# Keys and queries of heads 2, 4 and 6 by seven products ahead of attention 0, in place of gates; rotated operands split whole, stored and loaded as stacks

## The chip, the core and the metric

The kernel runs on one core of a Trainium2 chip, in one launch. The metric is the time of an execution on the device in microseconds (us); the median of three runs of the kernel before is 1436.19. The engines are TensorE (PE, with its weight loads as PEld), VectorE (DVE), ScalarE (ACT), GpSimd (POOL) and SyncE (SP), which issues the DMAs. Each executes its own instructions in order, and semaphores hold them together.

## The reference

A two-layer encoder trunk: 1024 tokens of width 1024, float32. Layer 0 is differential attention, layer 1 latent attention; each has an RMSNorm modulated by a conditioning vector, a SiLU gate, an output projection and a residual. The change lies in layer 0's projection and attention:

```python
# layer 0 (DA_HEADS 8, two parts of 64 per head, V of 128; D = SEQ = 1024)
proj = h @ w_in                                  # K, Q, V and the gate z, 1024 columns each
q, k, v, z = jnp.split(proj, [DA_WIDTH, 2 * DA_WIDTH, 3 * DA_WIDTH], axis=-1)
q = _rope(q.reshape(b, s, 2 * DA_HEADS, DA_QK_DIM), positions)
k = _rope(k.reshape(b, s, 2 * DA_HEADS, DA_QK_DIM), positions)
...
def block(qb):                                   # 128 queries
    sc = jnp.einsum('bqhcd,bkhcd->bhcqk', qb, k) * scale
    p = jax.nn.softmax(sc, axis=-1)
    p = p[:, :, 0] - lam * p[:, :, 1]
    return jnp.einsum('bhqk,bkhd->bqhd', p, v)
o = _rmsnorm(o, subln_g) * (1.0 - lambda_init)
o = o.reshape(b, s, DA_WIDTH) * jax.nn.silu(z)
return o @ w_out

def _rope(x, positions):                         # halves of 32 within each part of 64
    ...
    return jnp.concatenate([x1 * cos - x2 * sin, x2 * cos + x1 * sin], axis=-1)
```

## The kernel before

**Arithmetic.** Float32 is reached by splitting each operand into a high and a low part: `mm3` (L174 to L177) issues three matmuls per product, high x high, high x low, low x high. A split is an ACT cast to the high part and a subtraction for the low part, on POOL for weights (`split_raw`, L220 and L221, tiles `wh` and `wl`), on DVE for combinations and V. Operands are tiles of 128 partitions x 512 columns. The normalised input is `h0`, eight k-tiles by two token halves, each with a high and a low part (`h0h`, `h0l`).

**Head start.** `h0` is made, with the first half of V, K and Q of head 0 for the first token half beside it. The four last V tiles (`vacc`) are split and stored in memory (`store_v`, tiles `v_hl`, memory `vS`). Then K and Q of head 0 for the second token half, and the gate strip of head 6. A strip is one operand of one head: 1024 columns of weights by 128 rows, 16 steps of three matmuls. Raw K and Q of head 0 are parked in memory (`park`, `rS`).

**Pairs.** The gates of heads 0 to 5 are computed as three pairs of heads. A pair is a 2x2 block matrix product (two heads' weights, two halves of k) that takes seven products instead of eight: `z0_pair` (L931), with `product0` (L918: 12 matmuls into a PSUM tile `zacc`). It needs combinations of `h0` (`combos0`, L865: `tc`, `td` sums, `t1f` to `t4f`, each split into `t1..h`, `t1..l` and so on; L873 is the low part) and sums of weights (`z0_weights`, L902: L911 to L914 on DVE, then splits). `combos0` goes k by k, T1, T2, T4, T3 for each of the four k. PSUM tiles `acc` and `zacc` come in turn from five banks (`bank`, L117). Results go through SiLU (`gate_out`, L833) and are stored in `zS`.

**K1 and V.** After the pairs, the K strip of head 1 (16 steps, `Z_PRE`) and the second half of V, eight tiles of 24 matmuls (`v0_tile`, tiles `vps`). V's weights for it (`wv1`) are split there, with the low part on DVE (L554, L555). Beside it run the ropes of K and Q of head 0, the modulation products of layer 1 (DVE, `ada`, L441), and the first query tile (`V_LATE = 6`).

**Attention 0.** Per head and 128 queries: scores in PSUM (`s`, L1026, from the stacks `ks`, `qa`, `qb`), maximum (`nm`, DVE), exponential (`e`, ACT), the combination of both parts (L1034, DVE), transposes (`tr`), their splits (`pth` on ACT, `ptl` on DVE), then `pv` matmuls. Stream 0 supplies the strips of later heads as filler between them: `FILL0`, `FILL7` say how many steps go where. Its 15 strips are the rest of K and Q and the last gate.

**Ropes.** `rope` (L326) copies a strip out of PSUM (`rp_raw`), moves the 32-row blocks by four DMAs (`rp_sw`), multiplies by cosine and sine and adds (`rp_r`): three operations, on POOL but for head 0. Then `stack_k` (L358) and `stack_q` (L366) make the stacks: high and low parts of one 64-row half above each other, by two ACT casts and two POOL subtractions of 64 x 512, with four DMAs between halves for Q. What comes late is put in a side queue (`side.add`) whose jobs are called one per step (`side.tick`).

A scheduler places each engine's instructions by the order in which the code is written and its own priorities; `in_turn` and `behind` bind some of them. So the order on an engine is fixed when the kernel is built.

Of the kernel before, what the change touches and what calls it, by code (L numbers as in the profile page):

```python
# [11 lines left out]
F32 = mybir.dt.float32  # L12
# [27 lines left out]
FILL0 = ((1, 1, 1, 1, 1, 0), (1, 0, 1, 0, 1, 0)) * 3 + ((1, 1, 1, 1, 1, 0), (1, 0, 1, 0, 0, 0))  # L40
# [12 lines left out]
Z_PAIRS = 3  # L53
FILL7 = ((0, 1, 1, 1, 1, 0), (0, 1, 1, 1, 0, 0))
# [28 lines left out]
def trunk(ctx: ExitStack, tc: tile.TileContext, A, out):  # L83
# [54 lines left out]
    rS = dr.tile([2, 2, P, HF], F32, name="rS")  # L138
# [187 lines left out]
    def rope(rp, acc, half, scale, eng=G, add=V, parked=None):  # L326
# [5 lines left out]
        src = raw if parked is None else parked  # L332
        if parked is not None:
            SP.dma_start(raw, parked)
        elif scale == 1.0:
            S.copy(raw, acc)
        else:
            S.mul(raw, acc, scale)  # L338
        for q in range(4):
            SP.dma_start(sw[q * 32 : q * 32 + 32], src[(q ^ 1) * 32 : (q ^ 1) * 32 + 32])  # L340
# [17 lines left out]
    def stack_k(t, r):  # L358

        with behind("S"):  # L360
            S.copy(t[0:64, 0, :], r[0:64])
            S.copy(t[64:128, 1, :], r[64:128])
        in_turn(G.tensor_sub(t[64:128, 0, :], r[0:64], f32v(t[0:64, 0, :])))
        in_turn(G.tensor_sub(t[0:64, 1, :], r[64:128], f32v(t[64:128, 1, :])))

# [10 lines left out]

    def store_v(l, sp, acc, tt, fh, tag="vst", bufs=None):
        v = sp.tile([P, 2, HF], F32R, name="v_hl", tag=tag, bufs=bufs or VB[l])
# [376 lines left out]
    for tt in range(4):  # L755
        store_v(0, p1, vacc[tt], 4 + tt, 0, "xt", 6)

    def v0_tile(tt, fh, wv):
# [6 lines left out]
        if tt < V_LATE:  # L765
            store_v(0, p1b, acc, tt, fh)
        else:
            store_v(0, pm, acc, tt, fh, "ada", 3)
# [3 lines left out]

    def k_done(h):
        def f(acc, half, parked=None):
            rot, fin = rope(wp, acc, half, 1.0, *[G if h else V] * 2, parked)

            def g():
                t = a0a.tile([P, 2, HF], F32R, name="ks", tag="ks", bufs=4)
                stack_k(t, r.pop() if r else fin())
                KS.setdefault(h, [None, None])[half] = t  # L780

            r = []
            sum_ = [lambda: r.append(fin()), None] if h else []
            side.add(*[None] * ROT, rot, *[None] * (DEF - 1 - ROT), *sum_, g)
        return f

    def q_done(h):
        def f(acc, half, parked=None):
            rot, fin = rope(wp, acc, half, SC0, *[G if h else V] * 2, parked)

            def g():
                qa = a0a.tile([P, 2, HF], F32R, name="qa", tag="qs", bufs=4)
                qb = a0a.tile([P, 2, HF], F32R, name="qb", tag="qs", bufs=4)
                stack_q(qa, qb, r.pop() if r else fin())
                QS.setdefault(h, [None, None])[half] = qa, qb

            r = []
            sum_ = [lambda: r.append(fin()), None] if 0 < h < 5 else []
            side.add(*[None] * ROT, rot, *[None] * (DEF - 1 - ROT - (h == NH - 1)), *sum_, g)
        return f  # L800
# [8 lines left out]

    def z_done(h):  # L810
        def f(acc, half):
            GZ.setdefault(h, [None, None])[half] = silu_gate(wp, acc)
        return f

    def strip0(kind, h):
        return lambda: fetch_strip([A["w_s0"][kind, h, f] for f in range(2)], [4, 4])

    items = []
    for h in range(NH):
        items += [(strip0(1, h), h0, k_done(h)), (strip0(0, h), h0, q_done(h))]  # L820
# [1771 lines left out]
```

## Time and profile before

| what | us |
|---|---|
| runs | 1435.16, 1436.19, 1439.64 |
| profiled execution, its time | 1439.12 |
| its span | 1437.3 (mean granted clock 0.989) |
| head start | 0 to 81 |
| K0, Q0 second half, gate of head 6 | 81 to 103.1 |
| pairs | 103.1 to 180.1 |
| K1, second half of V | 180.1 to about 245 |
| first pv of attention 0 | 259.8 |

The profiled execution took 2.9 us more than the median, and 1.8 us of its time lie outside the span. The profile gives times in us from the span's start. A timeline row is: start, duration, engine, line, operation, output <- inputs, shape; in brackets the idle time of the engine just before it, and what ended it. A windows row is: window and length, busy time of each engine with the count of instructions, granted TensorE clock as a share, share of time in which the DMA engines worked, GB/s. A row of waits is: engine, what waited, line <- what it waited for: total, times, longest.

### The profile page before, as it was taken

The page shows a single profiled execution, that of the slowest core. Times are in us where ns is not written, and L with a number is a line of the kernel's source. Part 1 is how long each engine was busy: PE and PEld are TensorE (multiplying, and loading weights), DVE is VectorE, ACT ScalarE, POOL GpSimd, SP SyncE. Part 2 cuts the span into 40 slices and gives each one's busy share as a digit, 9 for nine tenths or more (in the row PEclk, how much of TensorE's full clock was granted, in tenths as well). Part 3 has the DMA queues.
Part 4 walks back from the last instruction along what each step waited for, and adds up shares of the span by engine and source line. Part 5 has one row for each costly group of instructions (what it writes and reads, how often), then busy time and mean ns, then how long its engine had stood idle before and what let it go on. Part 6 is the DMA issues. An engine that isn't in the chain of part 4 may idle for free.

```text
span 1437.3 us, 20898 instructions
## 1 busy us (share of the span) xinstructions
PE 1373.7 (96%) x7298; PEld 1141.9 (79%) x7298; DVE 986.8 (69%) x1392; ACT 760.2 (53%) x1369; POOL 773.2 (54%) x601
## 2 busy tenths in 40 slices
PE   8996989999999899999899899999999999999998
PEld 6774867878788788888787788887888888888886
DVE  7677564888787678777867886654655555555584
ACT  5533332656667566666754653334544454455554
POOL 5433434565598688876587232533032173753773
PEclk9997999999999999999999999999999999999999
DMA  9842267644544535444484236479544355565473
GB/s 342 285 128 74 73 216 221 202 135 125 147 131 156 172 110 173 149 138 120 145 322 154 67 72 204 170 248 269 160 132 120 107 135 194 193 220 191 134 269 117
DMA packets 154571, 241.50 MB, mean 168 GB/s; under 512 B 21217, under 2 KB 58209, under 8 KB 154466
## 3 DMA queue, kind: packets, MB, share of 16 engines
q1 hardware_dynamic: 154466, 240.18, 52.6%
q8 instruction: 57, 0.93, 0.3%
q14 instruction: 48, 0.39, 0.1%
HBM read 150.51 MB, written 66.53 MB: 151 GB/s over the span
## 4 chain that ended last, share of the span: by engine, by line
PE 60%; DVE 6%; ACT 3%; DMA 2%; issue 1%; POOL 1%; SPq 0%; POOLq 0%; ACTq 0%; DVEq 0%
PE s L2206 10%; PE tr L400 6%; PE acc L177 5%; PE acc L176 5%; PE s L1026 5%; PE acc L175 5%; PE pv L175 3%; PE pv L177 3%; PE pv L176 3%; PE oy L175 1%; PE oy L176 1%; PE oy L177 1%; PE zacc L177 1%; PE zacc L175 1%; PE zacc L176 1%
## 5 line engine op out<-in xcount | busy, mean ns | idle before, releaser
L402 ACT CAST pth<-tr 128x512 fp32r<-128x512 f32 x256 | 150.2, 587 | 250.2 <-PE tr L400 247.1
L403 DVE TENSOR_TENSOR ptl<-tr,pth 128x512 fp32r<-128x512 f32 x256 | 176.0, 687 | 144.7 <-ACT pth L402 139.9
L417 DVE TENSOR_REDUCE nm<-s 128x1 f32<-128x1024 f32 x192 | 233.6, 1217 | 18.5 <-PE s L1026 9.2
L221 POOL TENSOR_TENSOR wl<-wraw,wh 128x512 fp32r<-128x512 f32 (+2 forms) x65 | 83.9, 1292 | 204.4 <-ACT wh L220 155.0
L419 ACT ACTIVATE e<-s,nm 128x1024 f32<-128x1024 f32 x128 | 143.5, 1121 | 58.8 <-DVE nm L417 58.6
L400 PE MATMUL tr<-ident,e 128*128 128x128 f32 x1024 | 155.9, 275 | 6.0 <-DVE ptl L403 5.7
L400 PEld LDWEIGHTS tr<-ident,e 128*128 128x128 f32 x1024 | 121.2, 141 | 46.8 <-DVE ptl L403 25.8
L176 PE MATMUL pv<-ptl,vt 128*128 128x256 f32 x512 | 148.5, 290 | 0.7 <-DVE ptl L403 0.7
L175 PE MATMUL pv<-pth,vt 128*128 128x256 f32 x512 | 147.2, 288 | 0.4 <-ACT pth L402 0.4
L177 PE MATMUL pv<-pth,vt 128*128 128x256 f32 x512 | 144.6, 282 | 0.0
L175 PE MATMUL acc<-h0h,wh 128*128 128x512 f32 x264 | 108.8, 412 | 0.8 <-ACT wh L220 0.7
L177 PE MATMUL acc<-h0h,wl 128*128 128x512 f32 x264 | 104.5, 396 | 1.8 <-POOL wl L221 1.8
L176 PE MATMUL acc<-h0l,wh 128*128 128x512 f32 x264 | 104.2, 395 | 0.0
L221 POOL TENSOR_TENSOR wl<-zraw,wh 128x512 fp32r<-128x512 f32 (+2 forms) x39 | 56.8, 1461 | 85.5 <-ACT wh L220 82.2
L175 PEld LDWEIGHTS pv<-pth,vt 128*128 128x128 f32 x512 | 97.3, 190 | 3.8 <-ACT pth L402 1.9
L176 PEld LDWEIGHTS pv<-ptl,vt 128*128 128x128 f32 x512 | 97.6, 191 | 2.6 <-DVE ptl L403 1.1
L1026 PE MATMUL s<-ks,qa 128*128 128x512 f32 x256 | 86.0, 416 | 12.9 <-DVE e L1034 10.7
L1369 POOL TENSOR_TENSOR wol<-wol,woh 128x512 fp32r<-128x512 f32 x56 | 82.2, 1489 | 29.3 <-ACT woh L1368 26.4
L177 PEld LDWEIGHTS pv<-pth,vt 128*128 128x128 f32 x512 | 97.6, 191 | 0.2
L1026 PE MATMUL s<-ks,qb 128*128 128x512 f32 x256 | 83.7, 401 | 0.0
L1034 DVE SCALAR_TENSOR_TENSOR e<-s,z,e 128x1024 f32<-128x1024 f32 x64 | 82.2, 1284 | 2.2
L341 POOL TENSOR_TENSOR rp_r<-rp_raw,cosT 128x512 f32<-128x512 f32 x36 | 48.7, 1354 | 53.0 <-ACT rp_raw L338 52.3
(580 smaller groups left out, 3683.5 us busy)
## 6 DMA issues: line engine op xcount, KB each, us to landing
ada<-in_ada_ss SPq DMA_DIRECT2D x32, 512.0 KB, 6.1
vS<-v_hl SPq DMA_DIRECT2D x32, 512.0 KB, 6.0
vt<-vS SPq DMA_DIRECT2D x32, 512.0 KB, 4.8
wol<-tS SPq DMA_DIRECT2D x56, 256.0 KB, 5.4
wraw<-in_w_s SPq DMA_DIRECT2D x52, 256.0 KB, 2.8
tS<-ob SPq DMA_DIRECT2D x48, 256.0 KB, 2.1
rp_sw<-rp_raw SPq DMA_DIRECT2D x144, 64.0 KB, 2.0
bc_s<-bc_d SPq DMA_DIRECT2D x34, 256.0 KB, 3.9
```

The lines of the kernel that those rows point to most:

```text
L175: PE.matmul(psum, ah, bh, start=first, stop=False, skip_group_check=skip)
L176: PE.matmul(psum, ah, bl, start=False, stop=False, skip_group_check=skip)
L177: mm3.last = PE.matmul(psum, al, bh, start=False, stop=last, skip_group_check=skip).ins
L221: sub = (V if pair_of else G).tensor_sub(l_[:, :n], raw[:, :n], f32v(h_[:, :n]))
L400: transpose_p.last = PE.transpose(tr[:, j, :], p[:, kt * P : (kt + 1) * P], ident).ins
L402: mk["S"] = S.copy(pth[kh][:, :, dst], tr).ins
L403: mk["V"] = V.tensor_sub(ptl[kh][:, :, dst], tr, f32v(pth[kh][:, :, dst])).ins
L417: mk["V"] = V.reduce_max(nm, s_ps, axis=AX.X, negate=True).ins
L419: mk["S"] = S.activation(e, s_ps, AF.Exp, bias=nm, scale=1.0, accum_out=zs).ins
L1026: PE.matmul(s_ps[:, kc * HF : (kc + 1) * HF], src[:, c, ql], KS[h][kc][:, c, :], start=fst, stop=not fst)
L1034: combined.append(V.scalar_tensor_tensor(out=e0, in0=e1, scalar=z1[:, 0:1], in1=e0, op0=ALU.mult, op1=ALU.add).ins)
L2206: PE.matmul(s_ps[:, kc * HF : (kc + 1) * HF], lhs, rhs(kc), start=i == 0, stop=i == 4)
```

## The change

The pairs now compute K and Q of heads 2, 4 and 6 (`FRONT`), a head's K and Q being the two heads of the old pairs. The gate of head 0 takes the place of that of head 6 ahead of them. Stream 0 keeps 15 strips: K and Q of heads 1, 3, 5, 7 and gates 1 to 7 (`ORDER0`), with other filler counts. All gates are parked in `zS` and loaded for their head.

`rot_job` rotates a 128 x 512 operand as before and splits it whole: one cast on ACT, one subtraction for the low part; both parts go to memory (`hS`). `load_k` and `load_q` load the stacks from there by DMA. The ropes of heads 0 and 2 run on DVE during the pairs (8 jobs of 4 operations), those of heads 4 and 6 on POOL during V's second half (8 jobs), and those of the stream on POOL.

`combos0` does T1 and T2 of all k first, with the weight sums of the first pair after k = 1, then T3 of all k, then T4. Its temporaries get 12 tiles (8 before) and the weights 6 (8 before). The V tiles at the end of the head start are stored from `p1b` (tag `vst`, three buffers) and not from `p1` (tag `xt`, six). The second-half V weights are fetched and split at the end of the last pair, low part on POOL; they and V's stores live in `tp`, in the 16 buffers `tk` that hold the split combinations.

```diff
-FILL0 = ((1, 1, 1, 1, 1, 0), (1, 0, 1, 0, 1, 0)) * 3 + ((1, 1, 1, 1, 1, 0), (1, 0, 1, 0, 0, 0))
+FILL0 = ((1, 1, 1, 1, 1, 0), (1, 0, 1, 0, 1, 0)) * 4
+FILL6 = ((1, 1, 1, 1, 0, 0), (1, 0, 1, 0, 1, 0)) * 2 + ((1, 1, 1, 0, 1, 0), (1, 0, 1, 0, 0, 0)) * 2
-Z_PAIRS = 3
-FILL7 = ((0, 1, 1, 1, 1, 0), (0, 1, 1, 1, 0, 0))
+FRONT = (2, 4, 6)
+ORDER0 = ((1, 1), (0, 1), (2, 1), (1, 3), (2, 2), (0, 3), (2, 3), (1, 5), (2, 4), (0, 5), (2, 5), (1, 7), (2, 6), (0, 7), (2, 7))
+FILL7 = ((0, 1, 1, 1, 0, 0), (0, 1, 1, 1, 0, 0))
...
+    def rot_job(kind, h, half, eng, raw=None):
...
+        def first_():
+            b["r"] = rpt("rp_r")
+            turn_(eng.tensor_mul(b["r"], b["raw"], cosT[:, cs]))
+        def second():
+            turn_(eng.tensor_mul(b["sw"], b["sw"], sinT[:, cs]))
+            turn_(eng.tensor_add(b["r"], b["r"], b["sw"]))
+        def high():
+            with behind("S"):
+                S.copy(b["sw"].bitcast(F32R), b["r"])
+        def low():
+            turn_(eng.tensor_sub(b["raw"].bitcast(F32R), b["r"], b["sw"]))
+            for l_, t in enumerate((b["sw"], b["raw"])):
+                SP.dma_start(hS[kind][h][half][l_], t)
+        return fetch, first_, second, high, low
...
     for tt in range(4):
-        store_v(0, p1, vacc[tt], 4 + tt, 0, "xt", 6)
+        store_v(0, p1b, vacc[tt], 4 + tt, 0)
...
+    def load_k(h):
+        KS[h] = [a0a.tile([P, 2, HF], F32R, name="ks", tag="ks", bufs=4) for _ in range(2)]
+        for half, t in enumerate(KS[h]):
+            v = slots(1, h, half)
+            SP.dma_start(f32v(t[0:64]), v[:, 0::3])
+            for c in range(2):
+                SP.dma_start(f32v(t[64:128, c, :]), v[:, 2 - c])
...
+        for k in range(4):
+            V.tensor_sub(c_[k], d_[k], c_[k])
+            later(3, k, c_[k])
+            yield
+        for k in range(4):
+            bh, bl = parts[k][1]
+            V.tensor_sub(t2[k], bh, t2[k])
+            V.tensor_add(t2[k], t2[k], bl)
+            later(4, k, t2[k])
             yield
...
         if not p:
             side.flush()
+            add_jobs([(kind, 0, half) for kind in (1, 0) for half in range(2)] + [(kind, FRONT[0], half) for kind in (1, 0) for half in range(2)], V)
...
+    def split_v1(n):
+        for _ in range(n):
+            raw = wvraw.pop(0)
+            h_, l_ = tk()
+            S.copy(h_, raw)
+            G.tensor_sub(l_, raw, f32v(h_))
+            wv1.append((h_, l_))
...
+        if i < 2:
+            fetch_v1(2)
+        if i == 2:
+            split_v1(2)
+        if i == 3:
+            fetch_v1(2)
+            split_v1(2)
+            fetch_v1(2)
+            split_v1(4)
...
     stream0.step(Z_PRE)
+    add_jobs([(kind, h, half) for h in FRONT[1:] for kind in (1, 0) for half in range(2)], G)
...
-            if l == 0 and (h, half) >= (NH - 2, 1):
+            if l == 0:
                 hooks.append(lambda: hooks.append(scale))
...
+    def bring(h, i):
+        if h and i == 0:
+            load_q(h, 1)
+        if h < NH - 1 and i == 4:
+            load_k(h + 1)
+        if h < NH - 1 and i == 7:
+            load_q(h + 1, 0)
```

How this moves instructions, at three places. The first is the first pair, on **DVE, before**: the end of the combinations; `zs` and `zraw` (L911 to L914) are the weight sums, `z` the first add on a product.

```order
L892 TENSOR_TENSOR t4f<-h0h_0_143,t2f 128x512
L873 TENSOR_TENSOR t23l<-t2f,t23h 128x512
L893 TENSOR_TENSOR t4f<-t4f,h0l_0_144 128x512
L896 TENSOR_TENSOR t3f<-td,tc 128x512
L912 TENSOR_TENSOR zraw<-zraw 128x512
L873 TENSOR_TENSOR t43l<-t4f,t43h 128x512
L913 TENSOR_TENSOR zraw<-zs_1138,zraw 128x512
L873 TENSOR_TENSOR t33l<-t3f,t33h 128x512
L914 TENSOR_TENSOR zraw<-zraw 128x512
L936 TENSOR_TENSOR z_1165<-zacc,zu 128x512
```

**DVE, first pair, after**: lines L949 to L968 are the combinations, L937 the low parts (`tk`), L981 to L984 the weight sums.

```order
L981 TENSOR_TENSOR zs_1036<-zraw 128x512
L949 TENSOR_TENSOR tc<-h0h_1_188,h0l_1_189 128x512
L982 TENSOR_TENSOR zraw<-zraw 128x512
L950 TENSOR_TENSOR t1f<-tc,h0h_0_186 128x512
L937 TENSOR_TENSOR tk<-t1f,tk 128x512
L937 TENSOR_TENSOR tk<-t2f,tk 128x512
L937 TENSOR_TENSOR tk<-t1f,tk 128x512
L983 TENSOR_TENSOR zraw<-zs_1036,zraw 128x512
L951 TENSOR_TENSOR t1f<-t1f,h0l_0_187 128x512
L984 TENSOR_TENSOR zs_1037<-zraw 128x512
L937 TENSOR_TENSOR tk<-t2f,tk 128x512
L954 TENSOR_TENSOR td<-h0h_1_204,h0l_1_205 128x512
```

The weight sums now stand among the first combinations of k = 2, and no longer behind all combinations; the last of them (`zs_1037`) is the 14th row behind the fourth V tile (`v_hl`). The second place is the third pair, on **DVE, after** (before, only adds on `zacc`, gates and weight sums stood there):

```order
L393 TENSOR_TENSOR rp_sw<-rp_sw,sinT 128x512
L390 TENSOR_TENSOR rp_r<-rp_raw,cosT 128x512
L394 TENSOR_TENSOR rp_r<-rp_r,rp_sw 128x512
L401 TENSOR_TENSOR rp_raw<-rp_r,rp_sw 128x512
L393 TENSOR_TENSOR rp_sw<-rp_sw,sinT 128x512
L1010 TENSOR_TENSOR z_1623<-zacc,zu 128x512
L981 TENSOR_TENSOR zs_1537<-zraw 128x512
L982 TENSOR_TENSOR zraw<-zraw 128x512
L390 TENSOR_TENSOR rp_r<-rp_raw,cosT 128x512
L983 TENSOR_TENSOR zraw<-zs_1537,zraw 128x512
L394 TENSOR_TENSOR rp_r<-rp_r,rp_sw 128x512
L984 TENSOR_TENSOR zs_1538<-zraw 128x512
```

Rope operations (`rp_r`, `rp_sw`, `rp_raw`) now stand between the adds and among the third pair's weight sums. The third place is the stretch of K1 and V, on **POOL, before**, from the last splits of the pairs on:

```order
L221 TENSOR_TENSOR wl<-zraw,wh 128x512 x2
L221 TENSOR_TENSOR wl<-wraw,wh 128x512 x2
L346 TENSOR_TENSOR rp_sw<-rp_sw,sinT 128x512 x3
L221 TENSOR_TENSOR wl<-wraw,wh 128x512 x2
L363 TENSOR_TENSOR ks<-rp_r,ks 64x512
L364 TENSOR_TENSOR ks<-rp_r,ks 64x512
L363 TENSOR_TENSOR ks<-rp_r,ks 64x512
L364 TENSOR_TENSOR ks<-rp_r,ks 64x512
L371 TENSOR_TENSOR qb<-rp_r,qa 64x512
L372 TENSOR_TENSOR qb<-rp_r,qa 64x512
```

**POOL, after**: `tk<-wvr` are V's weights, `wl<-wraw` those of the strips K1 and the next.

```order
L224 TENSOR_TENSOR wl<-zraw,wh 128x512 x2
L1055 TENSOR_TENSOR tk<-wvr,tk 128x512 x3
L224 TENSOR_TENSOR wl<-wraw,wh 128x512
L1055 TENSOR_TENSOR tk<-wvr,tk 128x512 x4
L224 TENSOR_TENSOR wl<-wraw,wh 128x512
L1055 TENSOR_TENSOR tk<-wvr,tk 128x512
L224 TENSOR_TENSOR wl<-wraw,wh 128x512 x2
L390 TENSOR_TENSOR rp_r<-rp_raw,cosT 128x512 x2
L393 TENSOR_TENSOR rp_sw<-rp_sw,sinT 128x512
L394 TENSOR_TENSOR rp_r<-rp_r,rp_sw 128x512
L401 TENSOR_TENSOR rp_raw<-rp_r,rp_sw 128x512
L393 TENSOR_TENSOR rp_sw<-rp_sw,sinT 128x512
```

V's weight splits now stand ahead of and between K1's two, and the rope jobs follow in a chain. On **ACT, after**: `tk<-vps` are V's results, `rp_sw<-rp_r` the high parts of the rope jobs, `e` and `s` the exponentials.

```order
L412 CAST tk<-vps 128x512
L398 CAST rp_sw<-rp_r 128x512
L452 ACTIVATE s,z_2230<-s,nm 128x1024
L412 CAST tk<-vps 128x512
L398 CAST rp_sw<-rp_r 128x512
L452 ACTIVATE s,z_2335<-s,nm 128x1024
L398 CAST rp_sw<-rp_r 128x512 x4
L818 ACTIVATE rp_raw<-acc 128x512
L398 CAST rp_sw<-rp_r 128x512
L452 ACTIVATE e,zz<-s,nm 128x1024
L435 CAST pth<-tr 128x4x128 x2
```

and on **ACT, before**:

```order
L336 COPY rp_raw<-acc 128x512
L379 CAST v_hl<-vps 128x512
L336 COPY rp_raw<-acc 128x512
L369 CAST qa<-rp_r 64x512
L370 CAST qa<-rp_r 64x512
L379 CAST v_hl<-vps 128x512 x4
L419 ACTIVATE e,zz<-s,nm 128x1024
L379 CAST v_hl<-vps 128x512
L419 ACTIVATE s,z_2052<-s,nm 128x1024
L361 CAST ks<-rp_r 64x512
L362 CAST ks<-rp_r 64x512
L419 ACTIVATE e,zz<-s,nm 128x1024
```

Five of the rope casts now stand ahead of the second query tile's exponential (the row above the first `pth`), where the casts of stacks stood between V's results.

More of the change, by code (lines that the diff above doesn't have):

```diff
@@ L324, in step, with rope @@
                 side.tick()
[L326 removed]
+    def rope(rp, acc, half, scale, eng=G, add=V):
         cs = slice(half * HF, half * HF + HF)
@@ L764, in v0_tile @@
             mm3(acc, hh[:, c_], hl[:, c_], wv[k][0], wv[k][1], k == 0, k == KT - 1)
[L765 to L768, printed above, removed]
+            side.tick()
+        store_v(0, tp, acc, tt, fh, "tk", 16)
     KS, QS, GZ = {}, {}, {}
[L773 to L800, printed above, removed]
     def silu_gate(tp, acc):
@@ L980, in trunk, with late @@
-    assert not side.q and next(zw, None) is None
-    stT0.close()
+    def late(p, i):
+        if p + 1 < len(FRONT):
+            if i < 2:
+                z0_fetch(p + 1, ((i, 0), (i, 1)))
+            return
+        if i == 0:
+            z1raw = [raw_of(*ORDER0[0], f) for f in range(2)]
+            pre.append(z1raw)
+        if i < 2:
+            fetch_v1(2)
[6 more added lines that the diff above has]
+            split_v1(4)
@@ L1487, in extra0 @@
             side.flush()
+            for half in range(2):
+                load_gate(NH - 1, half)
             stW.close()
```

269 lines of the change are left out of this document (159 added, 110 removed).

## The prediction

> **What bounds the kernel now.** I read the page first: TensorE (PE) is busy almost throughout, so only the places where it stands still, or runs at a lower clock, can be won back.
>
> ```profile
> PE 1373.7 (96%) x7298; PEld 1141.9 (79%) x7298; DVE 986.8 (69%) x1392; ACT 760.2 (53%) x1369; POOL 773.2 (54%) x601
> ```
>
> Then the windows view, cut at the stages that the change touches: the seven-product pairs (103.1 to 181), K1 and the second half of V (181 to 240), most of attention 0 (300 to 700), and two cuts inside the first pair.
>
> ```profile
> 103.10:181.00 77.90, 63.01 (x257) 50.48 (x256) 51.46 (x74) 28.43 (x50) 33.96 (x22) 0.89 0.22 71
> 181.00:240.00 59.00, 53.54 (x230) 42.14 (x229) 29.75 (x42) 16.90 (x29) 25.77 (x18) 1.00 0.64 198
> 300.00:700.00 400.00, 381.05 (x2175) 319.31 (x2174) 310.78 (x444) 254.63 (x449) 292.65 (x238) 0.99 0.49 144
> 110.00:120.00 10.00, 3.77 (x10) 2.47 (x10) 10.00 (x17) 3.08 (x5) 0.00 (x0) 0.72 0.30 105
> 120.00:130.00 10.00, 4.85 (x11) 3.37 (x12) 5.96 (x11) 3.40 (x6) 4.19 (x3) 0.50 0.16 53
> ```
>
> Columns: length, then busy time of PE, PEld, DVE, ACT, POOL, granted clock, DMA. The pairs are the worst stretch of the three. In its first pair DVE is busy 10.00 of 10 us while PE works 3.77, and the granted clock is 0.72, then 0.50. The timeline says what a product costs and when the stage begins and ends:
>
> ```profile
> 103.12 0.39 PE L175 MATMUL zacc<-h0h,wh 128*128 128x512 f32 x1
> 105.84 0.39 PE L175 MATMUL zacc<-h0h,wh 128*128 128x512 f32 x1
> 109.97 0.50 PE L177 MATMUL zacc<-h0h,wl 128*128 128x512 f32 x1 [3.52 <-POOL wl L221]
> 125.01 0.79 PE L175 MATMUL zacc<-h0h,wh 128*128 128x512 f32 x1 [11.24 <-ACT wh L220]
> 180.11 0.39 PE L175 MATMUL acc<-h0h,wh 128*128 128x512 f32 x1
> ```
>
> The second row starts 12 matmuls after the first, so a product of 12 takes 2.72 us (0.227 each) and 21 take 57.1. The stage takes 180.11 - 103.12 = 77.0. So 19.9 us are lost: 14.8 in the two bracketed waits, some 5 at the low clock. Why the waits came:
>
> ```profile
> 84.65 0.69 DVE L883 TENSOR_TENSOR tc<-h0h,h0l 128x512 f32<-128x512 f32 x1 [1.77 <-DMA vS<-v_hl]
> 90.53 0.69 DVE L884 TENSOR_TENSOR t1f<-tc,h0h 128x512 f32<-128x512 f32 x1 [5.19 <-DMA vS<-v_hl]
> 120.02 0.68 DVE L893 TENSOR_TENSOR t4f<-t4f,h0l 128x512 f32<-128x512 f32 x1
> 120.62 0.68 DVE L896 TENSOR_TENSOR t3f<-td,tc 128x512 f32<-128x512 f32 x1
> 123.63 0.68 DVE L914 TENSOR_TENSOR zraw<-zraw 128x512 f32<-128x512 f32 x1
> 124.34 1.14 ACT L220 CAST wh<-zraw 128x512 fp32r<-128x512 f32 x2 [2.39 <-DVE zraw L914]
> ```
>
> DVE's combinations stood 6.96 us behind stores of V whose tiles lie in the same memory; they then run back to back, one per 0.60 us, with the weight sums last (L914 at 123.63, the cast at 124.34, PE at 125.01). And the 3.52 us wait:
>
> ```profile
> 103.42 6.50 POOL L221 TENSOR_TENSOR wl<-zraw,wh 128x512 fp32r<-128x512 f32 x1 [9.03 <-ACT wh L220]
> 108.11 0.67 DVE L888 TENSOR_TENSOR td<-h0h,h0l 128x512 f32<-128x512 f32 x1
> 108.72 0.67 DVE L807 SCALAR_TENSOR_TENSOR gz<-zth,acc 128x512 f32<-128x512 f32 x1
> 109.31 1.15 DVE L889 TENSOR_TENSOR t2f<-td,t1f 128x512 f32<-128x512 f32 x1
> 125.04 1.28 POOL L221 TENSOR_TENSOR wl<-zraw,wh 128x512 fp32r<-128x512 f32 x1 [15.12 <-ACT wh L220]
> ```
>
> POOL's split takes 1.28 us alone and took 6.50 here: it ended 1.2 us after DVE left its run of operations with two SBUF inputs for one whose input is in PSUM (L807), and the DVE operation behind that took 1.15 instead of 0.67.
>
> **The change, part by part.**
>
> ```profile
> L441 DVE CUSTOM_DVE_ANT_0 ada<-ada,c,vec 128x1024 f32<-128x1024 f32 x13 | 20.6, 1585 | 0.0
> ```
>
> This row (attention 0, by groups) prices the modulation products that stand among the rows counted next.
>
> *Combinations reordered.* V's stores now use a pool of their own, with three buffers for four tiles. Six combination rows run ahead of the fourth V tile, which has to wait for the first store. The first of the old waits ended at 84.65, the second at 90.53; I take about 86 for the fourth tile, and both as ends. The weight sums stand 14 rows behind it: 86 + 14 x 0.60 = 94.4, against 123.6 before and a need near 108. The 11.24 us wait goes, and so does the clock's fall after it. What is late next is the combination queue itself. Up to the add of the second product there are 47 DVE rows: 86 + 28 = 114, and with some five POOL splits let in between at 0.5 to 1.3 us each, 117 to 121. The last T4 split stands right behind that add, and products go to five banks in turn, so the seventh product needs both; its ideal start is 103.1 + 6 x 2.72 = 119.4. That leaves 0 to 4 us of stall, 2 taken.
>
> *32 rope operations on DVE inside the pairs* (heads 0 and 2, eight jobs of four). Before, DVE had room here: 51.46 busy of 77.90. From the second product's add to the weight sums of the third pair there are now 54 rows, 52 at 0.60 and two modulation products: about 34 us. That is 119 + 34 = 153. The splits of some 13 products come between them. Where a split enters beside an operation that reads PSUM, it costs DVE 0.5 (1.15 - 0.67); with no overlap it costs 1.28. So the sums end at 159 to 170. The 17th product needs them, and with 2 us of stall would be due at 103.1 + 16 x 2.72 + 2 = 148.6. Five products follow (13.6): the pairs end at 173 to 184 (180.11 before). Without any such delay, and were the rope rows overtaken, the end is 103.1 + 57.1 = 160.2. The price of this crowding is not in the old trace, since DVE was never full past the first pair, so I keep 160 to 184, and take 174, at the cheaper end of the crowded case: DVE also pauses for PE's products, and POOL enters then for nothing. Gain: 6 us (-20 to +4).
>
> The Trainium skill has a rule on this in "SBUF — State Buffer", section "Who interferes with whom": a DVE instruction with two SBUF inputs and a GpSimd instruction that reads SBUF share one port pair, and the second is fully blocked. The 6.50 against 1.28 agrees. Taken strictly it lets nothing overlap, which is the end at 184; the sum by it would be 10 us worse than mine.
>
> *V's weights split on POOL at the end of the last pair instead of on DVE after it.* Waits of the old K1 and V stretch:
>
> ```profile
> PE vps L175 <- DVE v_hl L380: 2.6, 2, 2.4
> PE vps L175 <- ACT wvh L554: 1.8, 1, 1.8
> PE vps L176 <- DVE wvl L555: 1.0, 1, 1.0
> 225.07 1.28 POOL L372 TENSOR_TENSOR qb<-rp_r,qa 64x512 fp32r<-64x512 f32 x1
> 226.44 1.29 POOL L341 TENSOR_TENSOR rp_r<-rp_raw,cosT 128x512 f32<-128x512 f32 x1
> 259.81 0.29 PE L175 MATMUL pv<-pth,vt 128*128 128x256 f32 x1
> ```
>
> The waits of 5.4 us go with their causes. In their place K1's second weight split stands behind seven V splits on POOL; at one POOL operation per 1.37 us (225.07 to 226.44) it is ready some 7 us after K1 starts, and K1's fifth step wants it after 4 x 3 x 0.227 = 2.7. So +4 against -5: net -1 (-5 to +5).
>
> *Ropes of heads 4 and 6 on POOL during V's second half.* With K1's two they are 10 jobs, 39 operations: 53 us at 1.37. The third job's low part waits for a cast that ACT has behind the sixth V tile, at T + 11 + 6 x 24 x 0.227 = T + 44 (T: end of the pairs); 28 operations follow, so POOL ends near T + 82. ACT has the last casts of these jobs ahead of the exponentials of attention's second tile, and the first pv behind those: about T + 83. Before it came at 259.81 = T + 79.7. DMA stores of the rotated halves stand ahead of V's stores and V's loads on SP's queue. PE gets some cover: one strip of 48 matmuls (10.9 us) now lies ahead of the first pv. I take +3 (-4 to +16).
>
> *Attention 0.* The stacks now come by DMA from memory half a head ahead, instead of by ACT casts and POOL subtractions just in time.
>
> ```profile
> PE s L1026 <- DVE e L1034: 10.4, 9, 4.8
> 499.93 1.10 PE L1026 MATMUL s<-ks,qa 128*128 128x512 f32 x2 [4.77 <-DVE e L1034]
> L371 POOL TENSOR_TENSOR qb<-rp_r,qa 64x512 fp32r<-64x512 f32 x14 | 18.0, 1284 | 9.7 <-ACT qa L369 9.7
> L363 POOL TENSOR_TENSOR ks<-rp_r,ks 64x512 fp32r<-64x512 f32 x14 | 18.0, 1287 | 41.3 <-ACT ks L361 40.6
> L361 ACT CAST ks<-rp_r 64x512 fp32r<-64x512 f32 x14 | 8.6, 613 | 7.9 <-POOL rp_r L348 7.9
> ```
>
> Four such POOL groups (4 x 18.0 us) and four ACT groups (4 x 8.6) go; about 14 whole-tile splits (18 and 9 us) come, and 14 gate products on DVE (9 us), which was 78% busy here (310.78 of 400). Neither engine is the bound, so only PE's waits count. Of the 19 us of waits in this stretch, 10.4 are for e; the longest (4.77) ended a rope chain that stood ahead of the exponential on ACT. I take 6 back (bounds -15 and +3, the last for the DVE work). The extra DMAs (from 1033 SP rows to 1173) I cost at nothing: the DMA engines are half busy there (0.49); were that cover gone, the loads have half a head, about 30 us.
>
> **Sum**, against the profiled execution of 1439.1: -6 - 1 + 3 - 6 = -10, or 1429. The median of the runs is 2.9 lower, 1436.2, so I forecast 1427.
>
> **Rivals.**
> - *More comes back* (0.2). Splits fit into DVE's pauses, the pairs end near 163, attention returns 8: -17 - 1 + 2 - 8 = -24, about 1413. For it: 20 us are plainly lost, and DVE could wait where PE has nothing to wait for. Against it: 90 DVE rows between 86 and 150.
> - *The stall moves and does not go* (0.2). Full blocking: the pairs end at 180 or later, with PE waiting for the third pair's weight sums instead of the first's: 0 - 1 + 3 - 5 = -3, about 1433 to 1438. The clock would fall again at that wait.
> - *Rope backlog delays attention 0: slower* (0.2). POOL's chain and the casts on ACT hold the first pv back. If the chain ends at T + 97 instead of T + 82 (each cast one V tile later, or V's loads landing behind the stores), PE runs out of the strip and waits 15 us more: -10 + 15 = +5, about 1441 to 1446. It decides from a first pv later than about T + 93. For it: ACT executes in order, four of those casts stand together ahead of an exponential. Against: V's work gives POOL 55 us of cover.
> - *The forecast* (0.4): 1421 to 1432.
>
> A rule of the Trainium skill bears on the second rival ("TensorE: Matmul & The Clock Gate", section "What's actually happening": after an idle window of about 3.4 us the gate passes half the pulses). The row of 0.50 behind the 11.24 us wait agrees.
>
> **Chances and range.** Under 0.3% (1431.9 to 1440.5 is no change, about what runs of this kernel can tell): all of the first rival and nearly all of the forecast's case make it faster, 0.55; the second rival and the forecast's upper edge are the same, 0.25; the third is slower, 0.2. The range leaves a tenth at each side: 1412 to 1443.
>
> **What would show it.** Right: no wait over 8 us in the first pair; 0 to 4 us before the seventh product; waits for POOL or ACT at the third pair's weights; first acc matmul of K1 at 170 to 177; a K1 wait of some 4 us for wl; first pv 80 to 86 us after that; waits for e under 6 us in all. Wrong: a pair stage under 62 us (crowding costs nothing) or over 77; a first pv past T + 93; or new waits in attention for ks or qa loads.

## The result, and the profile after

The change makes the kernel slower: median 1459.13 us (1458.04 to 1461.61, four runs) against 1437.91 for the kernel before beside it; ratio 1.0144, interval 1.0108 to 1.0181. The forecast was 1427. The profiled execution took 1461.6, its span is 1459.8 (before 1437.3): 22.5 us to explain.

The windows of the changed kernel, cut at the same stages (length, busy PE, PEld, DVE, ACT, POOL, clock, DMA share, GB/s):

```profile
103.00:181.00 78.00, 58.90 (x221) 44.73 (x220) 65.10 (x83) 27.26 (x49) 30.95 (x19) 0.87 0.59 193
181.00:240.00 59.00, 56.78 (x244) 46.52 (x243) 16.81 (x25) 14.76 (x27) 34.06 (x26) 0.97 0.69 190
240.00:300.00 60.00, 30.32 (x131) 23.82 (x130) 21.21 (x30) 16.46 (x29) 38.12 (x32) 0.77 0.82 249
300.00:700.00 400.00, 393.35 (x2273) 336.61 (x2273) 321.01 (x473) 237.68 (x422) 206.10 (x172) 0.99 0.71 204
150.00:160.00 10.00, 2.84 (x6) 1.83 (x7) 8.08 (x12) 3.11 (x5) 2.95 (x2) 0.67 0.82 264
```

In 300 to 700, most of attention 0, PE is busier than before (393.35 of 400 against 381.05). In the pairs it is less busy (58.90 of 78.00 against 63.01 of 77.90), and at the start of attention it works half of 60 us. The timeline of PE, with its larger waits and the ends of the stages (the first acc is K1's first matmul):

```profile
118.46 0.47 PE L178 MATMUL zacc<-tk,wh 128*128 128x512 f32 x1 [2.79 <-DVE zth L844]
157.03 0.79 PE L178 MATMUL zacc<-h0h,wh 128*128 128x512 f32 x1 [7.25 <-ACT wh L223]
171.46 0.80 PE L178 MATMUL zacc<-h0h,wh 128*128 128x512 f32 x1 [5.29 <-ACT wh L223]
188.69 0.39 PE L178 MATMUL acc<-h0h,wh 128*128 128x512 f32 x1
287.91 1.22 PE L1129 MATMUL s<-ks,qa 128*128 128x512 f32 x2 [25.55 <-ACT e L452]
299.29 0.35 PE L178 MATMUL pv<-pth,vt 128*128 128x256 f32 x1 [3.55 <-DMA vt<-vS]
```

And where the first matmul of the out projection stands, in the tile view of `oy` (min/median/max ns, first to last start), before and after:

```profile
L175 PE MATMUL oy<-woh,oah x136: 278/393/501, 694.8 to 1428.3; 128*128 128x512 f32 x132, 128*128 128x256 f32 x4
```

```profile
L178 PE MATMUL oy<-woh,oah x136: 278/393/505, 716.2 to 1450.5; 128*128 128x512 f32 x132, 128*128 128x256 f32 x4
```

So the difference at the end of attention is 21.4 us, in three parts. The pairs end at 188.69 instead of 180.11: +8.6. From there to the first pv: 110.6 instead of 79.7, +30.9. From the first pv to the out projection: 416.9 instead of 435.0, -18.1. After it the two kernels run alike (+22.2 at the last `oy`). Little of the -18.1 is work done earlier. These two windows rows, the first of the kernel before, count the strip matmuls (`acc`) from the pairs' end to the first pv (they have no column for POOL):

```profile
180.10:259.80 79.70, 20.19 (x83) 15.25 (x82) 0.00 (x0) 1.78 (x3) 1.00 0.71 224
188.68:299.28 110.60, 24.44 (x96) 18.85 (x95) 0.00 (x0) 2.39 (x4) 0.86 0.77 225
```

There were 83 and are 96 now. The 13 more are about 3.0 us at the 0.227 us that a matmul takes.

Why the large wait: the timeline of ACT and of POOL shows a chain of rope jobs, and the exponential that PE needs behind its last cast.

```profile
221.79 0.62 ACT L398 CAST rp_sw<-rp_r 128x512 fp32r<-128x512 f32 x1 [0.98 <-POOL rp_r L394]
261.86 0.62 ACT L398 CAST rp_sw<-rp_r 128x512 fp32r<-128x512 f32 x1 [7.66 <-POOL rp_r L394]
267.62 0.62 ACT L398 CAST rp_sw<-rp_r 128x512 fp32r<-128x512 f32 x1 [5.15 <-DMA rp_sw<-rS]
286.14 0.62 ACT L398 CAST rp_sw<-rp_r 128x512 fp32r<-128x512 f32 x1 [3.18 <-POOL rp_r L394]
286.66 1.11 ACT L452 ACTIVATE e<-s,nm 128x1024 f32<-128x1024 f32 x1
```

The first of the ten casts came at 221.79, the last at 286.14: 7.15 us a job on average, against 5.5 (four POOL operations at 1.37) in the forecast. And why the third pair waits, from SP's queue:

```profile
150.49 0.32 SPq L403 DMA_DIRECT2D hS<-rp_raw  x1
150.86 0.45 SPq L383 DMA_DIRECT2D rp_raw<-rS  x1
151.36 1.84 SPq L386 DMA_DIRECT2D rp_sw<-rS  x4
153.29 0.84 SPq L920 DMA_DIRECT2D zraw<-in_w_s  x2
156.36 1.26 ACT L223 CAST wh<-zraw 128x512 fp32r<-128x512 f32 x2 [1.00 <-DMA zraw<-in_w_s]
```

The first raw weights of the third pair are fetched at 153.29, behind rope stores (`hS`) and the loads that follow them; their cast comes at 156.36 and PE's matmul at 157.03. The rest is fetched at 159.40. The second wait, of 5.29 us, ends with the sums of these weights, and these stand on DVE behind an add on a product of the same pair, for which DVE waits until PE has made it:

```profile
166.28 0.69 DVE L1010 TENSOR_TENSOR z<-zacc,zu 128x512 f32<-128x512 f32 x1 [3.70 <-PE zacc L180]
166.89 0.68 DVE L981 TENSOR_TENSOR zs<-zraw 128x512 f32<-128x512 f32 x1
```

### The profile page after: what moved, and what is told of

The parts are those of the page before. It is cut to its first block, busy times and chain, and to the rows that moved or that the text cites. A ratio compares the mean times of both kernels' runs of the same rounds, so it can differ in the third digit from the quotient of the medians.

```text
span 1459.8 us, 20961 instructions
## 1 busy us (share of the span) xinstructions
PE 1379.5 (94%) x7298; PEld 1152.0 (79%) x7298; DVE 993.7 (68%) x1408; ACT 735.9 (50%) x1331; POOL 706.6 (48%) x553
## 4 chain that ended last, share of the span: by engine, by line
PE 51%; DMA 3%; DVE 3%; issue 2%; ACT 1%; POOL 1%; SPq 0%; POOLq 0%; DVEq 0%; ACTq 0%
PE s L2313 10%; PE tr L433 5%; PE acc L178 4%; PE acc L180 4%; PE acc L179 4%; PE pv L178 3%; PE pv L179 3%; PE pv L180 3%; PE s L1129 3%; PE zacc L178 1%; PE zacc L180 1%; PE zacc L179 1%; PE oy L180 1%; PE oy L178 1%; PE oy L179 1%
## 5 line engine op out<-in xcount | busy, mean ns | idle before, releaser
L224 POOL TENSOR_TENSOR wl<-zraw,wh 128x512 fp32r<-128x512 f32 (+2 forms) x36 | 51.6, 1440 | 77.2 <-ACT wh L223 57.3
L1129 PEld LDWEIGHTS s<-ks,qa 128*128 128x128 f32 x256 | 42.9, 192 | 41.5 <-ACT e L452 27.6
```

What stands on the lines that cost most here:

```text
L224: sub = (V if pair_of else G).tensor_sub(l_[:, :n], raw[:, :n], f32v(h_[:, :n]))
L1129: PE.matmul(s_ps[:, kc * HF : (kc + 1) * HF], src[:, c, ql], KS[h][kc][:, c, :], start=fst, stop=not fst)
```

## The experiments

Single profiled executions are named as such; the others are medians with the ratio to the kernel before beside them.

**1. Where the loss at the start of attention comes from.** The rope jobs of heads 4 and 6 in V's second half were first moved away, then done on another engine.

```diff
-    add_jobs([(kind, h, half) for h in FRONT[1:] for kind in (1, 0) for half in range(2)], G)
+    # in gen_strips0, at the first step of a gate strip:
+            if kind == 2 and gate_jobs:
+                add_jobs(gate_jobs[:2], G)
```

> The ropes of heads 4 and 6 leave V's second half and run two jobs per gate strip of stream 0 (gates 1 to 4); nothing else changes. Theory: PE's wait of 25.5 us ahead of the first pv comes from five rope casts that stand ahead of an exponential on ACT, each waiting for the chain of rope jobs on POOL. Then that wait goes (under 5 us), the first pv comes 80 to 86 us after the pairs' end (110.6 in the changed kernel), the time is 1432 to 1438. Rival: V's stores and loads or the full DMA engines (0.82 in that stretch) hold attention back: 15 us or more of the wait stay, 1448 or more.

Measured 1467.83, ratio 1.0216 (1.0185 to 1.0248). The wait goes, as theory had it: the first pv comes 74.4 us after the pairs' end.

```profile
189.09 0.39 PE L178 MATMUL acc<-h0h,wh 128*128 128x512 f32 x1
263.47 0.28 PE L178 MATMUL pv<-pth,vt 128*128 128x256 f32 x1
```

But the time does not fall, because attention 0 loses more than was won: PE is busy 369.88 of 400 there. The expected time failed; the place of the wait did not.

```diff
-    add_jobs([(kind, h, half) for h in FRONT[1:] for kind in (1, 0) for half in range(2)], G)
+    add_jobs([(kind, h, half) for h in FRONT[1:] for kind in (1, 0) for half in range(2)], V)
```

> The ropes of heads 4 and 6 stay in V's second half, on DVE instead of POOL. If POOL's four operations of 1.3 us set the pace of the chain (about 7 us a job), DVE at 0.6 ends it some 20 us sooner: wait ahead of the first pv 5 to 10 us, 1438 to 1444. If the two jobs in flight are paced by their round trip through memory (five loads issued, 3 us to land, store 2.3), a job still takes 5.5 to 6 us: wait 15 to 20, 1449 to 1455.

One execution: 1451.1. The wait falls from 25.5 to 19.0 only, so POOL's speed accounts for a quarter of it. Late in that chain some of DVE's rows wait for loads:

```profile
285.62 1.22 PE L1129 MATMUL s<-ks,qa 128*128 128x512 f32 x2 [19.04 <-ACT e L452]
275.89 0.69 DVE L393 TENSOR_TENSOR rp_sw<-rp_sw,sinT 128x512 f32<-128x512 f32 x1 [2.13 <-DMA rp_sw<-rS]
278.82 0.69 DVE L390 TENSOR_TENSOR rp_r<-rp_raw,cosT 128x512 f32<-128x512 f32 x1 [0.90 <-DMA rp_raw<-rS]
```

A job takes three of six buffers, so two jobs are in flight; each must be loaded, rotated, cast and stored before its buffers serve the next but one. No run with more buffers was made, so their share in the wait is not shown.

```diff
+            if high_on is G:
+                in_turn(G.tensor_copy(b["sw"].bitcast(F32R), b["r"]))
+                return
             with behind("S"):
                 S.copy(b["sw"].bitcast(F32R), b["r"])
```

> The ropes of heads 4 and 6 stay in V's second half as in the changed kernel; only their high casts move from ACT to POOL (8 copies of 1.3 us), so that ACT's exponential no longer stands behind them. If the order on ACT alone held attention back, the wait for e goes and the first pv comes near 265 to 270: 1435 to 1442. If SP's queue is a second gate (V's last stores and V's loads stand behind the stores of these jobs), the wait moves to vt<-vS or stays, first pv 290 or later: 1450 to 1462.

One execution: 1457.5, wait 22.9. With the casts off ACT two other waits stand ahead of the same exponential:

```profile
280.98 0.60 ACT L821 ACTIVATE rp_raw<-acc 128x512 f32<-128x512 f32 x1 [25.70 <-POOL rp_raw L404]
285.07 1.11 ACT L455 ACTIVATE e<-s,nm 128x1024 f32<-128x1024 f32 x1 [3.50 <-DMA vS<-tk]
```

The raw copy of the next strip needs one of the six rope buffers, which the chain frees; and the exponential's own tile lies where V's split results were, so it waits for V's stores, which stand on SP behind the rope stores. Moving the rope stores off SP too:

```diff
-                SP.dma_start(hS[kind][h][half][l_], t)
+                (G if eng is G else SP).dma_start(hS[kind][h][half][l_], t)
```

> The ropes of heads 4 and 6 in V's second half, high casts on POOL, and now all stores of POOL's rope jobs issued from POOL's own DMA queue, so that V's stores and loads no longer stand behind them on SP. Theory: with the casts on POOL two gates were left, the third V-store wait on SP (ACT's exponential waited for vS<-tk) and the raw copy of the next Q strip on ACT, which waits for a rope buffer that POOL's chain frees (25.7 us). If SP was the larger one, the first pv comes near 265 to 275: 1436 to 1446. If the rope buffers are, it stays at 285 or later: 1450 to 1460.

One execution: 1464.1, 6.6 more than the execution without; the raw copy waits 25.1 us for its buffer, the first pv is at 301.1. So with eight jobs there, neither the casts on ACT nor the stores on SP alone hold attention back; the chain does, through whichever wait is left.

**2. Why the pairs end late.**

```diff
-            SP.dma_start(raw, A["w_s0"][1 - m, FRONT[p], f])
+            (S if p else SP).dma_start(raw, A["w_s0"][1 - m, FRONT[p], f])
```

> The raw weights of the second and third pair are fetched by ACT's DMA queue instead of SP's; nothing else changes. Theory: in the third pair PE waits 7.25 and 5.29 us because the fetch stands on SP behind stores of the rope jobs. Then the pairs end at 174 to 180 (188.7 in the changed kernel), the time is 1445 to 1451. Rival, the crowding of DVE and POOL that was forecast: the weight sums come no sooner, the pairs end at 184 or later, 1455 to 1460.

Measured 1453.91, ratio 1.0111 (1.0091 to 1.0131). The pairs end at 172.09, even below the expected 174, so the fetch on SP's queue cost 16.6 us there. PE's matmuls stand in the same order in both kernels, but DVE's operations do not: with the weights there sooner, the scheduler put the third pair's sums ahead of the adds that they stood behind (first row below; 166.89 in the changed kernel). The 16.6 us are both together. The first pv gains only 5.8: the rope chain is the later arm now, and PE waits 35.3 us for it. The time, 1445 to 1451 expected, gains less for that reason.

```profile
144.28 1.40 DVE L981 TENSOR_TENSOR zs<-zraw 128x512 f32<-128x512 f32 x1 [1.85 <-DMA zraw<-in_w_s]
172.09 0.39 PE L178 MATMUL acc<-h0h,wh 128*128 128x512 f32 x1
281.71 1.22 PE L1129 MATMUL s<-ks,qa 128*128 128x512 f32 x2 [35.29 <-ACT e L452]
293.54 0.55 PE L178 MATMUL pv<-pth,vt 128*128 128x256 f32 x1 [3.90 <-DMA vt<-vS]
```

> As the first of these, and head 2's ropes leave the pairs: its Q in V's second half on POOL (two jobs), its K in gate 1; heads 4 and 6 in gates 2 to 5. So DVE has 16 rope operations in the pairs, not 32, and SP fewer stores ahead of the third pair's raw weights. Theory: both losses of the changed kernel go, the pairs end at 165 to 174, the first pv 80 to 86 us later, 1414 to 1424. Rival: the pairs are held by the combinations and their port alone: they end at 183 or later, 1430 to 1436.

Its edit takes head 2's four jobs out of the pairs (`add_jobs` there for head 0 only) and gives gates 1 to 5 two jobs each but for two in V's half. Measured 1471.47, ratio 1.0238 (1.0204 to 1.0271). The pairs end at 177.77 (165 to 174 expected, with the raw weights still on SP) and the first pv is at 256.96, but ten jobs in gates cost still more than eight. The expected time failed for the same reason as in the first run.

**3. What a rope job costs in attention 0.** First suspicion: a cast directly behind its last rope operation stops ACT.

```diff
-                add_jobs(gate_jobs[:2], G)
+                side.add(fA, None, None, fB, a1, a2, None, b1, hA, lA, b2, None, None, hB, lB)
```

> As the run with the ropes of heads 4 and 6 in the gate strips, but the two jobs of a strip are interleaved so that two to three stream steps lie between the last rope operation and the high cast (none lay there). Theory: that run lost in attention 0 because ACT stood 4 to 5 us before such casts, with exponentials behind them. Then the waits for e fall from 14.8 us to under 7, attention 0 is busy as in the changed kernel (PE over 390 of 400 in 300 to 700), and the time is 1428 to 1438. Rival: more work on POOL, ACT or the DMA queue in attention 0 costs by itself: PE stays under 380 of 400, 1455 or more.

One execution: 1467.9. PE's waits for `e` from ACT between 300 and 700 fell from 10.3 to 6.4 us, but waits for `qb` rose from 0.9 to 6.1 and PE is busy 368.23 of 400. So the suspicion does not explain the loss.

> The gapped gate strips and the raw weights on ACT's queue together. Theory: both losses of the changed kernel are gone and its gain in attention 0 stays. Pairs end near 172, first pv near 250, 1410 to 1422. Rival: the gains do not add, because attention 0 then waits for ropes: 1430 or more.

Measured 1459.60, ratio 1.0130 (1.0104 to 1.0155): pairs end at 172.48, first pv at 252.57, and attention 0 gives it all back (370.14 of 400). Nor did other gates help:

> Raw weights on ACT's queue; of the eight rope jobs of heads 4 and 6 two (K of head 4) stay in V's second half, two each go to gates 1, 3 and 5, which stand ahead of K strips, with the gap before the high casts. Theory: in the two gapped runs attention 0 lost because rope jobs in gates 2 and 4 delayed the side queue of the Q strips right behind them, whose stacks are wanted three query tiles later (PE waited 9.9 and 5.7 us for qa, 6.1 and 2.2 for qb). Then those waits fall under 5 us in all, first pv near 252, 1420 to 1435. Rival: any rope job in attention 0 costs: waits for e, qa and vt as before, 1450 or more.

Measured 1465.27, ratio 1.0172 (1.0143 to 1.0201). With only two jobs in V's half PE still waits 9.0 us ahead of the first pv, behind an exponential that waits for V's stores, which follow rope stores on SP:

```profile
254.92 1.11 ACT L452 ACTIVATE e<-s,nm 128x1024 f32<-128x1024 f32 x1 [12.49 <-DMA vS<-tk]
```

The sibling with four jobs in V's half:

> The same with four jobs (K and Q of head 4) in V's second half and two each in gates 1 and 3. The chain of six jobs, at 7 us each from about 200, ends near 245, before the second tile's exponential. Theory: first pv 250 to 258 and less in attention 0: 1416 to 1432. Rival (any backlog in V's second half holds V's stores back): first pv 265 or later, 1440 or more.

One execution: 1457.5, first pv 273.0. What these share stands in the waits of SP's queue, here of the gapped run with raw weights on ACT's queue, in 300 to 700 (what waited, for what: us, times, longest):

```profile
SPq L403 <- ACT rp_sw L398: 61.5, 18, 9.7
SPq L403 <- POOL rp_raw L401: 26.7, 19, 3.4
```

For 88 us of 400 (34 in the changed kernel) SP stood before a rope store (L403) whose data were not made yet, and everything behind it on SP, the loads of stacks and of V, stood too. The same edit of the store's queue as above, on this run:

> As the run with gapped gate strips and raw weights on ACT's queue (1459.6), but the stores of the rope jobs are issued from POOL's queue and not from SP's. Theory: in attention 0 SP's queue stands before such stores until POOL and ACT have made the halves, and loads of stacks and V behind them come late (PE waited 9.9 us for qa, 2.2 for qb, 3.2 for vt). Then these waits fall under 4 us, PE is over 385 of 400 busy in 300 to 700, 1425 to 1440. Rival: ACT's and POOL's order, not SP's, costs attention 0: 1452 or more.

Measured 1429.26 (nine runs, 1420.60 to 1435.46), ratio 0.9926 (0.9901 to 0.9952): 30 us less by one edit, and faster than the kernel before. The stretch from the first pv to the out projection falls from 463.8 to 436.3. PE is busy 380.95 of 400, not the 385 expected. Its waits for `qa` (9.9) are gone; those for `qb` and `vt` rose from 0.5 and 3.2 us to 4.4 and 5.3.

```profile
300.00:700.00 400.00, 370.14 (x2039) 303.85 (x2039) 292.94 (x418) 217.87 (x391) 226.33 (x188) 0.97 0.69 201
```

```profile
300.00:700.00 400.00, 380.95 (x2165) 323.32 (x2164) 308.79 (x450) 235.00 (x418) 255.71 (x235) 0.98 0.71 211
```

These are the gapped run without and with its stores on POOL's queue. That the queue alone did it isn't shown. With the stores moved, the scheduler also ordered PE's, ACT's and DVE's instructions anew, PE's from 241.6 us on. And SP's waits as a whole did not fall: in 300 to 700 all its rows of waits add to 210 us without the edit and 215 with it, as others took the place of the stores'. A run with the old orders kept wasn't made.

The edit was repeated on the two runs with jobs in V's half:

> The run with two rope jobs in V's second half and two each in gates 1, 3 and 5, with the stores of rope jobs on POOL's queue. Theory (SP's queue was the second gate): the wait of 9 us ahead of the first pv goes, attention 0 is as in the run with stores on POOL or better, 1420 to 1432. Rival (POOL's chain as such): the wait ahead of the first pv stays, 1435 or more.

> The same with four jobs in V's second half and two each in gates 1 and 3. If SP was the gate: first pv near 250 to 256, 1416 to 1430. If six jobs of POOL's chain at 7 us each hold the rope buffers (and with them the raw copy on ACT ahead of the second tile's exponential) until about 255: first pv 262 or later, 1430 to 1445.

Measured 1433.60, ratio 0.9963 (0.9948 to 0.9978), and 1437.7 in one execution: 32 and 20 us less than the same kernels with stores on SP. But the first pv comes at 259.2 and 266.2, later than with no job in V's half (249.3), and PE still waits for `e` there (longest 4.3 and 10.7, where the theory had such waits gone). So the stores on SP, with the orders that go with them, were the larger part, and the chain is a smaller one, which grows with each job.

**4. What the new order of the combinations is worth.**

> As the one before, with the combinations k by k (T1, T2, T4, T3) and the first pair's weight sums behind them, as in the kernel before. Theory: the new order is worth most of the first pair's stall; with the old one PE waits 8 to 12 us in the first pair again and the pairs end at 180 to 186, 8 to 14 us later than in the one before. Rival: the earlier start of the combinations (V's stores in their own pool) was the gain and the order is worth little: the pairs end at most 4 us later.

One execution: 1455.8; pairs end at 180.43 against 172.48. (This kernel does not compute the reference: T4 is made in T2's place before T2 is split, so the products with T2 get T4's values. The operations and their number are the same, but T2's split stands behind T4's two operations, which may add to its delay.) The first pair's wait is back:

```profile
119.07 0.79 PE L178 MATMUL zacc<-h0h,wh 128*128 128x512 f32 x1 [10.82 <-ACT wh L223]
```

Yet the first pv comes at 252.6 in both kernels: there the 7.95 us are lost again before it. And this part in the kernel before, together with V's stores in their own pool (`combos0` and `z0_weights` of the change with gates in the pairs, 12 and 6 buffers, V's stores from `p1b`; no rope moves):

> The kernel before with one part of the change alone: the new order of the combinations, the weight sums after k = 1, V's stores in their own pool; gates stay in the pairs and no rope moves. Theory: the first pair's stall of 19.9 us goes but for some 3 us, since no rope stands on DVE there: the pairs end at 160 to 166 and the time is 1420 to 1428. Rival: what is gained there is lost at K1 and V (first pv no earlier than 250): 1432 or more.

Measured 1423.74 (1422.48 to 1425.64), ratio 0.9899 (0.9881 to 0.9917): the lowest median of the study. The pairs end 12.0 us sooner than before, but later than the 160 to 166 expected, as one wait of 4.8 us for POOL is left (third row). The first pv and the out projection (681.9 instead of 694.8) keep the gain. What the order and the stores' pool each give isn't separated here.

```profile
168.09 0.39 PE L175 MATMUL acc<-h0h,wh 128*128 128x512 f32 x1
246.16 0.29 PE L175 MATMUL pv<-pth,vt 128*128 128x256 f32 x1
PE zacc L177 <- POOL wl L221: 4.8, 1, 4.8
```

## Why the prediction was wrong

**The combinations: mechanism right, remains too small.** No wait over 8 us is left in the first pair. What is left came earlier and is larger than forecast: the wait of 2.79 stands ahead of the fifth product, for a gate operation on DVE (L844), and the seventh product starts at 125.60, 6.2 us behind the ideal, where 0 to 4 were forecast and 2 taken. In the kernel before, the part with the stores' pool is worth 12.0 us at the pairs' end, twice the 6 that the sum gave to the whole stage.

**The ropes on DVE in the pairs: a queue missing.** DVE was full as forecast (30.00 of 30 us between 110 and 140). The step that failed is that only DVE and POOL were counted. Each rope job also puts five loads and two stores on SP, and the third pair's raw weights stood behind four such jobs; the text saw stores ahead of V's on SP one stage later, and not here. That term was left out, and it measured 16.6 us, with the order on DVE that it brought: 188.69 instead of 172.09. That 172.09 lies beside the 174 taken is in part luck: the path worked out had the third pair's sums end at 159 to 170, and in that run they end at 154.60. What is lost there are eight smaller waits of PE, 9.2 us in all: for POOL's splits (4.3), for the gate operation on DVE (2.9) and for ACT's casts (2.0).

Between back-to-back DVE operations POOL's splits did get in at times, at a price:

```profile
103.65 1.78 DVE L937 TENSOR_TENSOR tk<-t1f,tk 128x512 fp32r<-128x512 f32 x1
103.16 1.72 POOL L224 TENSOR_TENSOR wl<-zraw,wh 128x512 fp32r<-128x512 f32 x1 [13.83 <-DVE tc L962]
```

Such a meeting cost DVE 1.1 us here (1.78 for an operation that takes 0.68 alone), between the forecast's bounds of 0.5 and 1.28. The rule of the Trainium skill ("SBUF — State Buffer", section "Who interferes with whom") is that a DVE instruction with two SBUF inputs and a GpSimd instruction that reads SBUF contend for one port pair, an exclusive lock, so that the one which comes second is fully blocked; the pair of rows agrees. The rival that the forecast priced at full blocking (the pairs gain nothing) named the wait that came, at the third pair's weights, for another reason.

**V's weights on POOL: right.** K1 waits 2.2 us for its second split (some 4 forecast), and the waits of 5.4 for V are gone.

**The ropes in V's second half: mechanism right, size wrong.** This was the third rival, with 0.2, at T + 97 and +5 in all. The first pv came at T + 110.6, for +30.9 instead of +3. The term that failed is the chain's end, T + 82 by 28 operations at 1.37 behind the third job's low part. On POOL, the third job's low part, two of the waits behind it, and the last low part:

```profile
237.73 1.29 POOL L401 TENSOR_TENSOR rp_raw<-rp_r,rp_sw 128x512 fp32r<-128x512 f32 x1 [2.35 <-ACT rp_sw L398]
248.39 1.30 POOL L393 TENSOR_TENSOR rp_sw<-rp_sw,sinT 128x512 f32<-128x512 f32 x1 [3.03 <-DMA rp_sw<-rS]
259.16 1.29 POOL L390 TENSOR_TENSOR rp_r<-rp_raw,cosT 128x512 f32<-128x512 f32 x1 [3.60 <-DMA hS<-rp_sw]
286.83 1.26 POOL L401 TENSOR_TENSOR rp_raw<-rp_r,rp_sw 128x512 fp32r<-128x512 f32 x1 [0.73 <-ACT rp_sw L398]
```

The third low part comes at T + 49 instead of T + 44, and from it to the chain's end at 288.1 (T + 99.4) go 50.4 us instead of 38.4. In these POOL waits 7.8 us for loads and stores and 5.6 for ACT's casts, and the sum had priced operations alone. The first pv comes 11.2 us behind the chain's end, where the sum had 1: V's last stores and then V's loads (at 293.65) stand behind the chain's on SP, which it had named and not priced. DVE in POOL's place gained 6.5 us of the wait and no more. The cover of one strip ahead of the first pv was for the most part there before (83 strip matmuls, now 96).

**Attention 0: direction right, size wrong.** -18.1, of which some 3.0 is work done earlier, leaves -15.1 against -6, at the edge of the bounds (-15 to +3). PE's waits for `e` from DVE fell from 10.4 to 2.4, as forecast; the rest isn't taken apart.

```profile
PE s L1129 <- DVE e L1137: 2.4, 3, 1.7
```

But this gain hangs on the jobs being done in V's half: done inside attention, with the stores on SP, the same rope jobs leave PE 23 us less busy in 400 (370.14 for 393.35).

**Sum, in the prediction's terms:** pairs +8.6 for -6, K1, V and start of attention +30.9 for +2, attention -18.1 for -6: +21.4 at the end of attention for -10. (From the median of 1436.2 the terms give 1426, not 1427.) The two large misses are work on queues that the sum did not price: SP's in the pairs, and the round through loads, casts and stores in V's half.

What stays open: why attention 0 still loses 19 us of PE in the best gated run (380.95 of 400) where the changed kernel loses 7; the places of the rope jobs and the engines' orders changed together there. Nor was it tried whether more rope buffers shorten the chain, or how much the order of the combinations gives without the stores' pool. The sum of the two gains (the new order, and gated ropes with stores on POOL) beyond the order alone wasn't found: 1429.3 does not beat 1423.7.

## What to carry to other kernels

For every step that is moved, write down its DMAs with the queue they are issued from, and what stands behind them on that queue: here a store that stood on SP's queue before its data existed held every load behind it. Where a chain of jobs shares a few buffers, price a job's loads, hand-overs between engines and stores too, and not only its operations. And try the part of a large change that removes a visible stall alone: here it was worth 1%, and the changed kernel, which has the rest too, takes 2.5% more than that part alone.

## What the hardware showed that was not expected

A store issued from POOL's own queue took 0.59 and 0.54 us of POOL's time (rows of the run with casts and stores on POOL). With the orders that came with it, that edit was worth 20 to 32 us in three kernels with rope jobs in gates; in the one with all eight jobs in V's half it cost 6.6 (two of these four differences are between single executions).

```profile
228.90 0.59 POOL L406 DMA_DIRECT2D hS<-rp_sw  x1
229.49 0.54 POOL L406 DMA_DIRECT2D hS<-rp_raw  x1
```

A cast of 128 x 512 on POOL took 0.61 us where its subtraction takes 1.26 to 1.29 (the run with high casts on POOL). And PE's waits of 5 to 7 us are paid twice: behind 7.25 and 5.29 us the first matmuls take 0.79 and 0.80 instead of 0.39, and the clock granted in 150 to 160 was 0.67. The Trainium skill's page "TensorE: Matmul & The Clock Gate" (section "What's actually happening") states that the clock is halved after an idle window of about 3.4 us; the doubled matmuls agree.
